# An expert layer on one core: one jump over the third block per group of weights instead of per product

## The chip, the cores and the metric

The kernel runs on one core of a Trainium2 chip. Its time is the device time in microseconds. The kernel before has a median of 1426.74 us over three runs (1427.4, 1422.75 and 1426.74).

## The reference

A trunk of two layers works on 256 tokens of width 1024, all in float32. Layer 0 is multi-scale retention and a dense SwiGLU; layer 1 is stick-breaking attention against a shared K and V, and then a mixture of eight experts. Each sub-layer ends in a layer norm over `alpha * x + f(x)`. The change is in the experts alone. There each token goes to the two experts with the largest router logits:

```python
top_val, top_idx = lax.top_k(logits, TOP_K)          # 2 of 8
gates = sum(one_hot(top_idx) * softmax(top_val))
for e in range(8):                                    # D_EXPERT = 3584
    gate, up = split(xt @ w_in[e])                    # 1024 x 7168
    y += gates[:, e] * ((silu(gate) * up) @ w_out[e]) # 3584 x 1024
```

The weights of the eight experts are 352 MB, and each is read once.

## The kernel before

Tokens are gathered per expert into 96 slots, in three blocks (`NB = 3`) of 32. An expert that has at most 64 tokens has nothing in its third block. That is known on the chip only: the router writes the flag `over[e]`, and TensorE loads it into a register (`third[e]`).

The 3584 hidden columns of an expert are worked in two units, of 2048 and 1536 (`UNITS`). For each unit `experts` runs three products: the gate and the up product (`gemm_e`, "input products", 8 weights each, a weight being 128 rows of the unit's columns) and the output product of the unit before (`down`, 16 or 12 weights of 128 rows by 1024 columns). So an expert has six products. In a product, a step is one weight: `mm_tiles` (L1102) multiplies, for each block of 32 slots, four column groups that lie side by side in the array, and each of these is two records in the profile. Between the units stand the scatter of the expert before (L1155 to L1161), and the gather of the next expert.

Weights go unsplit from HBM into slots of 1 MB. There are 18 slots in this stage (6 + 6 + 2 + 4, from four pools). A slot holds one weight of an input product (1 MB or 768 KB) or two of an output product (1 MB). All loads are issued by SP's queue (L213) in the order of use. A load waits there until the slot that it gets is given back by `done()`; `pump` hands slots to the next loads as they are given back.

`by_need` (L1105 to L1120) sets the order within a product. It takes the slots of the whole product, works the first weight with all three blocks and gives its slot back, works the other weights with the blocks 0 and 1, and then comes to one `tc.If(third > 0)` (L1118), in which the other weights are worked with block 2. Only then come the `done()` of all weights but the first. If the flag is zero, TensorE jumps over the third block's instructions. The very first product is worked weight by weight without a branch, since the flags are not loaded yet.

After the last expert follow the copies of the rows out of PSUM (L1146: blocks 0 and 1 on ScalarE, block 2 on VectorE), the last scatter, and the layer norm.

Of the kernel before, what the change touches and what calls it, by code (L numbers as in the profile page):

```python
# [24 lines left out]
KD = D // P  # L25
# [6 lines left out]
NB = 3  # L32
# [149 lines left out]
def trunk_kernel(ctx, tc, x, ret_w_in, ret_w_out, sb_w_kv, sb_w_q, sb_w_out, ln_mix_g, ln_mix_b,  # L182
# [17 lines left out]
    def wtile(name="pw"):  # L200
        return psw.tile([P, 512], F32, tag="pw", name=nm(name))
# [602 lines left out]
    def blocks(w):  # L804

        v = w.rearrange("p (b t j) -> p b t j", t=4, j=32)
        return [v[:, :, t, :] for t in range(4)]
# [13 lines left out]
    def gather_T(ps):  # L821

        xg = mp.tile([P, NB, KD, 32], F32, tag=("xgh", "xgl")[cnt_xg[0] % 2], name=nm("xg"))
        cnt_xg[0] += 1
        for r in range(NB):
            nc.vector.transpose(xg[:, r].rearrange("p k s -> p (k s)"), ps[r])
        return xg
# [14 lines left out]
    with att:  # L842
# [234 lines left out]
        xg = gather_T(first)  # L1077
# [17 lines left out]
    def mm_tiles(nb, o, lhs, cols, first, last, shared=False):  # L1095

        for r in nb:
            for c, w in enumerate(cols):
                ov = o[r][c * 32:(c + 1) * 32]
                if len(w.shape) == 3:  # L1100
                    ov = ov.rearrange("p (b j) -> p b j", j=32)
                nc.tensor.matmul(ov, lhs[r], w, start=first and not (shared and r == 1), stop=last,  # L1102
                                 skip_group_check=True)

    def by_need(s, nk, third, mm):  # L1105


        if third is None:
            for k in range(nk):
                mm(range(NB), k, s.take()[0])  # L1110
                s.done()
            return
        w = s.take(nk)
        for k in range(nk):
            mm(range(NB) if k == 0 else range(NB - 1), k, w[k])
            if k == 0:
                s.done()
        with tc.If(third > 0):  # L1118
            for k in range(1, nk):
                mm(range(NB - 1, NB), k, w[k])  # L1120
        for k in range(1, nk):
            s.done()

    def gemm_e(s, xg, n, third):


        o = [wtile("pe")[:, :n // 4] for _ in range(NB)]
        by_need(s, KD, third, lambda nb, k, w: mm_tiles(nb, o, [xg[:, r, k, :] for r in range(NB)], blocks(w),
                                                        k == 0, k == KD - 1))
        return o  # L1130

    def down(s, hT, nk, po, first, last, third):
        by_need(s, nk, third, lambda nb, k, w: mm_tiles(nb, po, [hT[:, r, k, :] for r in range(NB)],
                                                        [w[:, c * 256:(c + 1) * 256] for c in range(4)],
                                                        first and k == 0, last and k == nk - 1, True))

# [28 lines left out]
    def experts(s, pos, g, xg, norm, hook=None, most=None):  # L1165
        pend = done = po = None
        third = [None] * NE
        for e in range(NE):
            for u, (c0, n) in enumerate(UNITS):
                hs = mp2.tile([P, NB, 512], F32, tag="hs", name=nm("hs"))[:, :, :n // 4]  # L1170
                pg = gemm_e(s, xg, n, third[e])
                for r in range(NB):
                    nc.scalar.activation(hs[:, r, :], pg[r], AF.Silu)  # L1173
# [8 lines left out]
                if u == 1:  # L1182
# [3 lines left out]
                    if e + 1 < NE:  # L1186
                        g = one_hot(e + 1, pos)
                        nxt = gather(g)
                pu = gemm_e(s, xg, n, third[e])
                hT = xtp.tile([P, NB, 16, 32], F32, tag="xT_l", name=nm("hT"))[:, :, :n // P]  # L1190
                for r in range(NB):
# [3 lines left out]
                if pend is not None:  # L1195
                    if pend[1] == 0:
                        po = new_po()
                    down(s, *pend[0], po, pend[1] == 0, pend[1] == 1, third[e - (u == 0)])
                    if pend[1] == 1:
                        done = (rows_of(po), *sl)  # L1200
                pend = ((hT, n // P), u)
            if e + 1 < NE:
                xg = nxt
        down(s, *pend[0], po, False, True, third[NE - 1])
        scatter(rows_of(po), *sl, norm)

# [68 lines left out]
```

## Time and profile before

| what | value |
|---|---|
| profiled execution | 1422.93 us |
| its span | 1421.1 us |
| TensorE busy | 1349.7 us (95%) |
| mean granted TensorE clock | 0.974 |
| moved over DMA | 447.36 MB |
| expert stage | from about 537 us of the span to 1397 us |

The span goes from the first to the last instruction; the profiled execution's own time is 1.8 us longer. Times in the rows are counted from the span's start. A matmul record's line is that of the helper (L1102), so products are told apart by time, by tile (`pe` for input products, `po` for output products) and by their number of records. "PEq L1118" as a releaser is TensorE's sequencer at the branch of `by_need`.

### The profile page before, as it was taken

How to read it: one execution, taken by the hardware profiler on the slowest of the kernel's cores; microseconds unless marked ns; L12 is line 12 of the kernel's file. 1: busy time of each engine (PE TensorE's matmuls, PEld its weight loads, DVE VectorE, ACT ScalarE, POOL GpSimd, SP SyncE). 2: the span in 40 equal slices, each digit the busy share in tenths (PEclk: the TensorE clock that was granted, in tenths of full speed). 3: DMA queues.
4: the chain of work that ended last, by engine and by line, in shares of the span. 5: the costliest groups of instructions: out<-in, count | busy, mean ns of one | idle time of the engine just before them, and what ended most of it. 6: DMA issues, size and time to landing. Idle time of an engine off the chain costs nothing. (4 is left out here: it accounts for less than half of the span.)

```text
span 1421.1 us, 29884 instructions
## 1 busy us (share of the span) xinstructions
PE 1349.7 (95%) x13608; PEld 842.3 (59%) x13608; DVE 443.4 (31%) x617; ACT 314.2 (22%) x466; POOL 58.5 (4%) x80
## 2 busy tenths in 40 slices
PE   9999999999999999987989999999999999999894
PEld 7888879999989863533524444454444453443442
DVE  6746667555566570101201200200200200200204
ACT  5544425444447520001000000100100100100101
POOL 0212110000010020000000000000000000000001
PEclk9999999999999999999999999999999999999997
DMA  9864536655586356999999999989999999999960
GB/s 338 296 210 151 175 119 238 205 180 182 144 243 241 139 223 202 406 418 412 411 419 412 412 418 410 405 341 413 411 418 413 411 402 414 411 418 414 412 271 33
DMA packets 137251, 447.36 MB, mean 315 GB/s; under 512 B 9088, under 2 KB 56976, under 8 KB 120720
## 3 DMA queue, kind: packets, MB, share of 16 engines
q1 hardware_dynamic: 136144, 442.01, 80.9%
q0 software_dynamic: 960, 3.15, 0.7%
q8 instruction: 122, 2.00, 0.6%
q14 instruction: 25, 0.20, 0.0%
HBM read 444.08 MB, written 1.05 MB: 313 GB/s over the span
## 5 line engine op out<-in xcount | busy, mean ns | idle before, releaser
L1102 PE MATMUL pe<-raw,xg 128*32 128x512 f32 (+1 forms) x5304 | 513.3, 543 | 21.4 <-DMA raw<-in_moe_w_in_dram 9.6
L1102 PEld LDWEIGHTS pe<-raw,xg 128*32 128x32 f32 x5304 | 185.5, 110 | 339.6 <-issue 305.3
L1102 PE MATMUL po<-raw,hT 128*32 128x256 f32 x4544 | 249.9, 379 | 5.8 <-DMA raw<-in_moe_w_out_dram 3.3
L265 DVE TENSOR_TENSOR w<-raw,w 128x1024 fp32r<-128x1024 f32 x162 | 198.1, 1234 | 143.8 <-ACT w L264 139.8
L1102 PEld LDWEIGHTS po<-raw,hT 128*32 128x32 f32 x4544 | 158.0, 110 | 100.8 <-issue 7.4
L264 ACT CAST w<-raw 128x1024 fp32r<-128x1024 f32 x162 | 168.2, 1047 | 134.3 <-issue 32.1
L1192 DVE TENSOR_TENSOR hs<-hs,pe 128x512 f32<-128x512 f32 (+1 forms) x48 | 29.1, 620 | 384.0 <-PE pe L1102 382.6
L1173 ACT ACTIVATE hs<-pe 128x512 f32<-128x512 f32 (+1 forms) x48 | 25.4, 543 | 507.5 <-PE pe L1102 507.5
L393 PE MATMUL pf<-xT_h,w 128*128 128x256 f32 x448 | 126.9, 283 | 0.0
L395 PE MATMUL pf<-xT_l,w 128*128 128x256 f32 x448 | 126.2, 282 | 0.0
L394 PE MATMUL pf<-xT_h,w 128*128 128x256 f32 x448 | 126.1, 281 | 0.0
L1194 DVE STREAM_TRANSPOSE hT<-hs 128x512 f32<-128x512 f32 (+1 forms) x48 | 27.2, 617 | 230.0 <-PE po L1102 125.0
L393 PEld LDWEIGHTS pf<-xT_h,w 128*128 128x128 f32 x448 | 84.4, 188 | 0.3
L394 PEld LDWEIGHTS pf<-xT_h,w 128*128 128x128 f32 x448 | 84.4, 188 | 0.3
L395 PEld LDWEIGHTS pf<-xT_l,w 128*128 128x128 f32 x448 | 84.4, 188 | 0.0
L1146 ACT COPY y<-po 32x256 f32<-32x256 f32 x64 | 23.3, 364 | 258.4 <-PE po L1102 257.7
L456 POOL TENSOR_SCALAR rs<-mv 128x1 f32<-128x1 f32 x16 | 5.6, 350 | 1292.4 <-DVE mv L455 1284.5
L368 PE MATMUL pv<-w,xT_l 128*128 128x512 f32 x96 | 38.4, 400 | 0.0
L369 PE MATMUL pv<-w,xT_h 128*128 128x512 f32 x96 | 37.9, 395 | 0.0
L370 PE MATMUL pv<-w,xT_h 128*128 128x512 f32 x96 | 37.9, 395 | 0.0
L1156 DVE SCALAR_TENSOR_TENSOR yl<-y,gs,yh 96x512 fp32r<-96x512 f32 x16 | 11.9, 744 | 82.9 <-ACT yh L1155 82.8
L393 PE MATMUL pq<-xT_h,w 128*128 128x256 f32 x128 | 36.3, 283 | 0.0
(208 smaller groups left out, 1274.1 us busy)
## 6 DMA issues: line engine op xcount, KB each, us to landing
raw<-in_moe_w_in_dram SPq DMA_DIRECT2D x128, 1024.0 KB, 18.9
raw<-in_moe_w_out_dram SPq DMA_DIRECT2D x112, 1024.0 KB, 18.4
raw<-in_moe_w_in_dram SPq DMA_DIRECT2D x128, 768.0 KB, 15.2
raw<-in_ret_w_in_dram SPq DMA_DIRECT2D x22, 1024.0 KB, 9.1
raw<-in_ffn_w_in_dram SPq DMA_DIRECT2D x20, 1024.0 KB, 5.1
raw<-in_ffn_w_out_dram SPq DMA_DIRECT2D x11, 1024.0 KB, 5.0
raw<-in_ret_w_out_dram SPq DMA_DIRECT2D x8, 1024.0 KB, 5.0
raw<-in_sb_w_kv_dram SPq DMA_DIRECT2D x4, 1024.0 KB, 5.3
```

Source lines behind the costliest of these rows:

```text
L264: nc.scalar.copy(hv, v)
L265: nc.vector.tensor_sub(lv, v, hv.bitcast(F32))
L368: nc.tensor.matmul(o, sl, mh, start=first, stop=False)
L369: nc.tensor.matmul(o, sh, mh, start=False, stop=False)
L370: nc.tensor.matmul(o, sh, ml, start=False, stop=last)
L393: nc.tensor.matmul(o, lo[:, k, :], xT_h[:, k, :], start=(k == 0), stop=False)
L394: nc.tensor.matmul(o, h[:, k, :], xT_h[:, k, :], start=False, stop=False)
L395: nc.tensor.matmul(o, h[:, k, :], xT_l[:, k, :], start=False, stop=(k == KD - 1))
L1102: nc.tensor.matmul(ov, lhs[r], w, start=first and not (shared and r == 1), stop=last, skip_group_check=True)
L1173: nc.scalar.activation(hs[:, r, :], pg[r], AF.Silu)
L1192: nc.vector.tensor_mul(hs[:, r, :], hs[:, r, :], pu[r])
L1194: nc.vector.transpose(hT[:, r].rearrange("p k s -> p (k s)"), hs[:, r, :])
```

## The change

`by_need` gets a group size: 4 weights for input products and 8 for output products, which is four slots' worth in both. It goes through a product group by group. Each group is taken, worked with the blocks 0 and 1 (the product's first weight with all three), then passes a branch of its own, in which its weights are worked with block 2, and then gives its slots back. An input product has two groups of 4; an output product has two of 8, or one of 8 and one of 4. The number of matmuls and their operands stay; their order within a product changes, and a product has two branches instead of one.

```diff
@@ -1102,7 +1102,8 @@
                 nc.tensor.matmul(ov, lhs[r], w, start=first and not (shared and r == 1), stop=last,
                                  skip_group_check=True)
 
-    def by_need(s, nk, third, mm):
+    def by_need(s, nk, group, third, mm):
+
 
 
         if third is None:
@@ -1110,27 +1111,31 @@
                 mm(range(NB), k, s.take()[0])
                 s.done()
             return
-        w = s.take(nk)
-        for k in range(nk):
-            mm(range(NB) if k == 0 else range(NB - 1), k, w[k])
-            if k == 0:
+        for k0 in range(0, nk, group):
+            ks = range(k0, min(k0 + group, nk))
+            w = s.take(len(ks))
+            for k in ks:
+                mm(range(NB - (k > 0)), k, w[k - k0])
+            if k0 == 0:
                 s.done()
-        with tc.If(third > 0):
-            for k in range(1, nk):
-                mm(range(NB - 1, NB), k, w[k])
-        for k in range(1, nk):
-            s.done()
+            with tc.If(third > 0):
+                for k in ks:
+                    if k > 0:
+                        mm(range(NB - 1, NB), k, w[k - k0])
+            for k in ks:
+                if k > 0:
+                    s.done()
 
     def gemm_e(s, xg, n, third):
 
 
         o = [wtile("pe")[:, :n // 4] for _ in range(NB)]
-        by_need(s, KD, third, lambda nb, k, w: mm_tiles(nb, o, [xg[:, r, k, :] for r in range(NB)], blocks(w),
+        by_need(s, KD, 4, third, lambda nb, k, w: mm_tiles(nb, o, [xg[:, r, k, :] for r in range(NB)], blocks(w),
                                                         k == 0, k == KD - 1))
         return o
 
     def down(s, hT, nk, po, first, last, third):
-        by_need(s, nk, third, lambda nb, k, w: mm_tiles(nb, po, [hT[:, r, k, :] for r in range(NB)],
+        by_need(s, nk, 8, third, lambda nb, k, w: mm_tiles(nb, po, [hT[:, r, k, :] for r in range(NB)],
                                                         [w[:, c * 256:(c + 1) * 256] for c in range(4)],
                                                         first and k == 0, last and k == nk - 1, True))
```

## Rows read from the trace of the kernel before

**Rows 1.** Stage windows: us, busy time of each engine, TensorE clock, DMA share, GB/s.

```profile
550.00:560.00 10.00, 9.30 (x88) 3.12 (x84) 0.00 (x0) 1.77 (x3) 0.00 (x0) 1.00 0.76 240
560.00:570.00 10.00, 9.68 (x100) 3.65 (x96) 3.43 (x6) 0.00 (x0) 0.00 (x0) 1.00 0.18 46
570.00:580.00 10.00, 9.83 (x126) 4.99 (x122) 0.71 (x3) 1.79 (x5) 0.00 (x0) 1.00 1.02 419
...
1300.00:1310.00 10.00, 10.00 (x129) 3.90 (x125) 2.07 (x3) 0.00 (x0) 0.00 (x0) 1.00 1.02 414
...
1370.00:1380.00 10.00, 10.00 (x192) 5.59 (x188) 0.00 (x0) 0.00 (x0) 0.00 (x0) 1.00 0.55 191
```

**Rows 2.** TensorE's waits, 633 to 729.7 us: us in total, times, longest.

```profile
PE pe L1102 <- DMA raw<-in_moe_w_in_dram: 7.7, 13, 2.0
PE po L1102 <- DMA raw<-in_moe_w_out_dram: 3.3, 5, 0.7
```

**Rows 3.** TensorE's waits, 729.6 to 1397 us.

```profile
PE pe L1102 <- DMA raw<-in_moe_w_in_dram: 2.4, 3, 1.5
```

**Rows 4.** TensorE's timeline behind output products: start, us, what, records, idle before.

```profile
1051.59 43.10 PE L1102 MATMUL pe<-raw,xg 128*32 128x512 f32 x384 [3.15 <-PEq L1118]
...
1105.85 15.69 PE L1102 MATMUL pe<-raw,xg 128*32 128x384 f32 x192 [0.37 <-DMA raw<-in_moe_w_in_dram]
...
1263.78 3.16 PE L1102 MATMUL pe<-raw,xg 128*32 128x512 f32 x25 [0.32 <-PEq L1118]
1268.30 38.40 PE L1102 MATMUL pe<-raw,xg 128*32 128x512 f32 x356 [1.36 <-issue]
...
1319.42 15.69 PE L1102 MATMUL pe<-raw,xg 128*32 128x384 f32 x192 [1.50 <-DMA raw<-in_moe_w_in_dram]
```

**Rows 5.** Timeline of the load queue (SPq): start, us, loads, count.

```profile
567.27 2.50 SPq L213 DMA_DIRECT2D raw<-in_moe_w_in_dram  x5
...
1292.07 32.77 SPq L213 DMA_DIRECT2D raw<-in_moe_w_in_dram  x16
```

**Rows 6.** Loads of slots issued 1290 to 1332 us: time to landing.

```profile
DMA to landing us min/median/max: 14.7/16.2/19.0
```

**Rows 7.** TensorE's timeline: expert 0's second and third product, expert 2's first.

```profile
552.33 14.80 PE L1102 MATMUL pe<-raw,xg 128*32 128x512 f32 x136 [0.69 <-issue]
567.45 11.17 PE L1102 MATMUL pe<-raw,xg 128*32 128x384 f32 x136 [0.32 <-PEq L1118]
...
727.08 1.92 PE L1102 MATMUL pe<-raw,xg 128*32 128x512 f32 x16 [0.57 <-DMA raw<-in_moe_w_in_dram]
729.56 28.53 PE L1102 MATMUL pe<-raw,xg 128*32 128x512 f32 x264 [0.56 <-DMA raw<-in_moe_w_in_dram]
```

**Rows 8.** The load queue's own waits, 556 to 575 us.

```profile
SPq L213 <- PEq L1118: 11.7, 1, 11.7
```

**Rows 9.** DMA issues of the page: tensor, count, size, median us to landing.

```profile
raw<-in_moe_w_in_dram SPq DMA_DIRECT2D x128, 768.0 KB, 15.2
```

**Rows 10.** Timeline of TensorE: expert 3's first two products, in one piece.

```profile
833.73 41.39 PE L1102 MATMUL pe<-raw,xg 128*32 128x512 f32 x384
```

**Rows 11.** Timeline of TensorE: behind input products of experts 4 and 6.

```profile
1033.99 14.45 PE L1102 MATMUL po<-raw,hT 128*32 128x256 f32 x264 [0.18 <-PEq L1118]
...
1183.77 14.80 PE L1102 MATMUL pe<-raw,xg 128*32 128x512 f32 x136 [0.32 <-PEq L1118]
1199.06 15.75 PE L1102 MATMUL po<-raw,hT 128*32 128x256 f32 x288 [0.49 <-PEq L1118]
...
1249.01 14.45 PE L1102 MATMUL po<-raw,hT 128*32 128x256 f32 x264 [0.18 <-PEq L1118]
```

**Rows 12.** Timeline of all engines: copies of the last product's rows.

```profile
1392.36 3.01 ACT L1146 COPY y<-po 32x256 f32<-32x256 f32 x8 [49.54 <-PE po L1102]
1397.11 1.74 DVE L1146 COPY y<-po 32x256 f32<-32x256 f32 x4 [15.01 <-PE po L1102]
```

## The prediction

> **What bounds the kernel now.** I read the stage windows first, then TensorE's waits, then its timeline product by product, then the load queue. From about 570 us the DMA engines are saturated (share 1.02, 414 and 419 GB/s in [rows 1]), which looks like a memory bound. But a full queue does not show who is late. The waits tell it: between 633 and 729.7 us TensorE waited 7.7 + 3.3 = 11.0 us for weights [rows 2], between 729.6 and 1397 us only 2.4 us in three waits [rows 3], and even the longest of these, 1.50 us at 1319.42 [rows 4], is not for data: its product's first slot is the first of the 16 loads that begin at 1292.07 [rows 5], such loads land 14.7 to 19.0 us after issue [rows 6], so it was there by 1311; and no later slot of that product, which would land 1.9 us apart, was waited for. So there are two stretches. Until 729.56 the weight stream sets the time: slot after slot, TensorE idles for the next one (0.57 and 0.56 us in [rows 7]). From 729.56 to the end of the last product TensorE does, and what it does more or less there, and how early it gets there, is the span. The load stream ends at about 1376 (share 0.55 in the window 1370 to 1380 [rows 1]), some 20 us before TensorE.
>
> A product of 192 records (8 weights x 3 blocks x 4 columns x 2) ran the third block, one of 136 jumped over it. By that count experts 0, 1, 4 and 6 jump, and 2, 3, 5 and 7 don't.
>
> **The change part by part.**
> *Earlier loads.* Expert 0's second product starts at 552.33 and ends at 567.1 [rows 7]. Its slots are full, and the queue waits 11.7 us for the branch behind the product [rows 8]; then, at 567.27, five loads go out within 2.50 us [rows 5], and the DMA share of 560 to 570 is 0.18 [rows 1]. With the change the first group of four weights is done after 24 + 3 x 16 = 72 records of 14.80/136 = 0.109 us, so at 560.2, and three slots come free (the first already came free alone). Three loads of 768 KB = 0.786 MB [rows 9] at 415 GB/s ([rows 1]) are 5.7 us of transfer, and fit into the 7 us to 567.3. The queue then never runs dry: four more slots follow at 567.3 (8.8 us of loads), and the next product gives back halves too. The stream is 5.7 us further from there. The cover for this is the 11.0 us that TensorE waits before 729.56: these can shrink by 5.7, with a few new jumps (0.3 each, below) also inside them. Bounds: 0, if the three loads don't get out earlier, and 5.7, since there are only three slots. I take 5.7.
>
> *Blocks done while waiting.* Expert 2's first product runs the third block and waits for its weights. Now the last weight begins at 729.56, and behind it come two blocks and then seven third blocks. With groups, the third blocks of the weights 1 to 3 are done behind weight 3, while weights 4 to 7 still come in: three blocks of 8 x 28.53/264 = 0.865 us [rows 7], 2.6 us, are taken out from behind the last landing. They fit: weights 4 to 7 need 1.72 us of TensorE each at a landing every 2.5 us, so the 2.6 us is made up again before the last one. The product's end goes from 729.56 + 1.73 + 7 x 0.865 = 737.3 to about 729.0. The stream stays close for the next three products: the next one's last weight lands at 729.56 - 5.7 + 8 x 2.5 = 743.9, and TensorE comes to it at 729.0 + 2.6 + 3 x 1.73 + 2.6 + 3 x 1.73 = 744.6, which leaves 0.7 us. Bounds 0 and 2.6; I take 2.6. So TensorE gets to its own stretch 5.7 + 2.6 = 8.3 us earlier.
>
> *More jumps.* A product that runs its third block shows no gap at its branches: 384 records of two products in one piece, 41.39 us [rows 10], 0.108 us each as in a waitless stretch. So the added branches of experts 2, 3, 5 and 7 cost nothing, bound 0.3 each. A jump taken costs 0.18, 0.32, 0.49 and 0.18 us behind input products [rows 11], mean 0.3. These jump over 7 weights x 4 columns x 4 = 112 instructions (two records, each with its weight load). Each input product of experts 4 and 6 has one jump more (over 48, then 64): 8 x 0.3 = +2.4 us, all on the path. Those of experts 0 and 1 are in the first stretch, under the waits.
>
> *Shorter jumps.* Behind the output products, which jump over 15 x 16 = 240 or 11 x 16 = 176 instructions, the gaps are another thing [rows 4]: 3.15 us (expert 4), 0.37, then 0.32 and 1.36 a little later (expert 6), and 1.50. The 3.15 us also left TensorE slower: the next 384 records took 43.10 us instead of 41.39, 1.7 us more. Sum 3.15 + 1.7 + 0.37 + 1.68 + 1.50 = 8.4 us. With the change each becomes two jumps over 112 and 128, or 112 and 64, instructions. By the nearest rows, those of 112, that is 4 x 2 x 0.3 = 2.4 us: a gain of 6.0. The other end: the stalls stay as they are and each product has one short jump more, 4 x 0.3 = 1.2 us lost. I take the 6.0, since length is what differs between the two sets of rows, and keep both ends.
>
> [...]
>
> *The tail.* In the last product the copies of the first two blocks' rows (3.01 us on ScalarE) begin at 1392.36, under the last eleven third blocks; the third block's copies begin at 1397.11 [rows 12]. With groups of 8 and 4 the first two blocks end only four third blocks before the end, 4 x (1397.11 - 1392.36)/11 = 1.7 us, so ScalarE's copies end 0.4 us later than VectorE's first half does now: +0.4 us.
>
> **Sum.** -5.7 - 2.6 + 2.4 - 6.0 + 0.4 = -11.5 us on the profiled execution's 1422.93, 1411.4. The timed runs lie between 1422.75 and 1427.4, median 1426.74, so that execution is at their lower end, 3.8 below the median. I put half of this on top: 1413.
>
> **Rivals.**
> 1. *The long stalls are not of the length.* Then +1.2 instead of -6.0: 1418.6, and 1420.5 with half the difference to the median. For it: the four gaps of the output products differ among themselves by a factor of eight. Against: none of the rows of 112 comes near.
> 2. *The stream is not moved.* The three slots don't come back before the branch at the product's end, or the loads only wait later. Then -2.6 + 2.4 - 6.0 + 0.4 = -5.8: 1417.1, 1419 with the half. That is also the case in which the change does not do what it says. For it: a slot's return follows a branch, and how that is counted no row shows. Against: the returns at 567.27 follow the branch directly.
> 3. *Slower: every jump stalls.* If a branch in the middle of a product meets instructions not yet there, the 24 jumps of experts 4 and 6 (16 in input products, 8 in output products) cost what the long ones do now, (3.15 + 0.37 + 1.68 + 1.50)/4 = 1.7 us: 24 x 1.7 = 40 us, instead of the 2.4 + 6.7 = 9.1 that these products' jumps cost now. +31 - 8.3 + 0.4 = +23, 1446. It turns from faster to slower at (9.1 + 8.3 - 0.4)/24 = 0.7 us per jump. For it: there are twice as many jumps. Against: no jump over 112 instructions costs more than 0.49.
>
> **How the numbers follow.** Forecast 0.5, rival 1 0.22, rival 2 0.13, rival 3 and what lies between it and rival 1 0.15. A measurement of this kernel tells about 0.3%, 4.3 us, from no change, so faster means under 1422.5. The forecast and both first rivals are under it, with about a tenth of their chance not, by the spread of the runs. Of the last 0.15 a half is slower than 1431. Faster 0.78, the same 0.13, slower 0.09. The likeliest case's own range is 1406 to 1418; low end 1406 if the clock drops behind stalls (1.7 us at one of them) go elsewhere too; high end 1425 takes in rivals 1 and 2 and the start of the third.
>
> **What would show it.** Right: the DMA share of 560 to 570 well over half; no run of waits for weights in the second half of expert 2's first product, and its end near 729 instead of 737.3; experts 4 and 6 with two gaps of about 0.3 us in each product and none over 1 us; two-product pieces of 384 records still without a gap. Wrong: the share at 560 still near 0.2 (rival 2), gaps over 1 us behind the output products (rival 1) or in the middle of products (rival 3), or new waits for weights after 770, which would say that TensorE has caught the stream and part of the 11.5 us stays there.

## The result: 1419.47 us, 7 us under before

The changed kernel takes 1419.47 us (median of 7 runs, 1418.51 to 1420.67) against 1426.68 us for the kernel before (7 runs); the ratio is 0.995, with an interval of 0.994 to 0.996. The forecast of 1413 us had the direction and, as the experiments show, the mechanism of the earlier loads; its size was nearly twice what came. The time is that of the first rival (1418.6 to 1420.5), but by luck: the terms of its sum are not the ones that were measured, as the part on the prediction shows.

The stage windows of the changed kernel (columns as in [rows 1]) show the weight stream where it was idle before:

```profile
550.00:560.00 10.00, 9.32 (x92) 3.04 (x87) 0.00 (x0) 1.79 (x3) 0.00 (x0) 1.00 0.86 273
560.00:570.00 10.00, 9.62 (x88) 3.02 (x80) 0.78 (x2) 0.00 (x0) 0.00 (x0) 1.00 0.72 274
570.00:580.00 10.00, 9.72 (x120) 4.62 (x124) 3.37 (x7) 0.00 (x0) 0.00 (x0) 1.00 0.92 344
```

From 560 to 570 us the DMA share is 0.72, where it was 0.18. TensorE's waits for weights follow, first those of 633 to 730 us, then those of 729.6 to 1397 us (us in total, times, longest):

```profile
PE pe L1102 <- DMA raw<-in_moe_w_in_dram: 2.1, 6, 0.4
PE po L1102 <- DMA raw<-in_moe_w_out_dram: 0.4, 1, 0.4
...
PE pe L1102 <- DMA raw<-in_moe_w_in_dram: 1.6, 1, 1.6
PE po L1102 <- DMA raw<-in_moe_w_in_dram: 0.3, 1, 0.3
```

In the first stretch 11.0 us [rows 2] have become 2.5. TensorE's timeline shows the places that answer to [rows 4, 7, 10]:

```profile
709.74 16.66 PE L1102 MATMUL pe<-raw,xg 128*32 128x512 f32 x144 [0.31 <-PEq L1121]
726.71 25.96 PE L1102 MATMUL pe<-raw,xg 128*32 128x512 f32 x240 [0.30 <-DMA raw<-in_moe_w_in_dram]
...
765.12 11.82 PE L1102 MATMUL pe<-raw,xg 128*32 128x384 f32 x144 [1.27 <-PEq L1121]
778.51 4.08 PE L1102 MATMUL pe<-raw,xg 128*32 128x384 f32 x48 [1.58 <-DMA raw<-in_moe_w_in_dram]
...
830.67 41.39 PE L1102 MATMUL pe<-raw,xg 128*32 128x512 f32 x384
...
1047.80 41.41 PE L1102 MATMUL pe<-raw,xg 128*32 128x512 f32 x384 [0.30 <-PEq L1121]
...
1100.69 15.69 PE L1102 MATMUL pe<-raw,xg 128*32 128x384 f32 x192 [0.32 <-PEq L1121]
...
1256.73 5.56 PE L1102 MATMUL po<-raw,hT 128*32 128x256 f32 x97 [0.47 <-issue]
1263.10 41.41 PE L1102 MATMUL pe<-raw,xg 128*32 128x512 f32 x384 [0.81 <-PEq L1121]
...
1316.18 15.69 PE L1102 MATMUL pe<-raw,xg 128*32 128x384 f32 x192 [0.30 <-PEq L1121]
...
1396.20 0.50 PE L1164 MATMUL psc<-yh,gT 96*128 96x512 f32 x1 [2.15 <-ACT yh L1160]
```

Expert 2's first product (from 709.74) runs 144 records before its only wait, 0.30 us for the last weight. The 3.15 us behind expert 4's first unit are 0.30 now (1047.80), the 1.50 at the end are 0.30 (1316.18). But other gaps stand there: 1.27 us at 765.12, then a wait of 1.58 us for a weight at 778.51, and 0.47 and 0.81 us around 1260, where before had 0.32 and 1.36 [rows 4]. Expert 2's third product (an expert's input products are counted from first to fourth), which has the wait, was not free of gaps in before either:

```profile
769.21 1.45 PE L1102 MATMUL pe<-raw,xg 128*32 128x384 f32 x10 [0.33 <-PEq L1118]
771.16 15.04 PE L1102 MATMUL pe<-raw,xg 128*32 128x384 f32 x182 [0.49 <-issue]
```

A product that runs its third block still has no gap at its branches (830.67).

The profiled execution took 1420.67 us, 2.3 less than that of before, although the medians differ by 7.2. Part of that is ahead of the change: expert 0's second product starts at 554.61 here and at 552.33 in [rows 7]. So from here on places are counted from the start of that product. The start of each product is found in every run by counting the records of the trace, since the number of records of each product is known:

| kernel | expert 2, second product starts | expert 2, first output product starts | expert 4 starts | expert 6 starts | last product ends |
|---|---|---|---|---|---|
| before (us) | 185.0 | 260.7 | 401.1 | 616.3 | 844.7 |
| before, profiled again | +0.1 | +0.7 | +0.8 | +1.0 | +0.7 |
| changed | -7.7 | -5.3 | -5.0 | -6.3 | -5.3 |
| e0_only | -4.9 | -4.2 | -3.7 | -3.3 | -3.4 |
| in_only | -7.6 | -6.5 | -6.3 | -6.6 | -5.1 |
| out_only | +0.1 | +1.1 | +1.6 | +0.8 | +2.3 |
| shift_before | +0.8 | +1.2 | +1.3 | -1.9 | -2.7 |
| e2_only | -2.5 | +1.0 | +1.5 | +1.9 | +1.8 |
| early_in | -7.8 | -5.5 | -5.1 | -7.9 | -5.5 |
| finer | -8.0 | -5.9 | -5.8 | -3.5 | -3.4 |
| shift_256 | -0.1 | +0.9 | +1.6 | +2.1 | +2.1 |
| shift_after | -6.8 | -5.6 | -5.4 | -3.4 | -2.5 |
| e0_fine | -6.5 | -5.9 | -5.6 | -6.3 | -7.9 |
| early_in_long | -7.5 | -4.9 | -5.0 | -6.4 | -4.5 |

Every line after the first is that kernel's time less that of the first line, from one profiled execution each.

### The profile page after: what moved, and what is told of

It reads as the page before. It is cut to its first block, busy times and chain, and to the rows that moved or that the text cites. A ratio compares the mean times of both kernels' runs of the same rounds, so it can differ in the third digit from the quotient of the medians.

```text
span 1418.8 us, 30029 instructions
## 1 busy us (share of the span) xinstructions
PE 1353.8 (95%) x13608; PEld 849.3 (60%) x13608; DVE 443.4 (31%) x617; ACT 314.1 (22%) x466; POOL 58.6 (4%) x80
## 3 DMA queue, kind: packets, MB, share of 16 engines
q0 software_dynamic: 960, 3.15, 0.7%
## 5 line engine op out<-in xcount | busy, mean ns | idle before, releaser
L1102 PEld LDWEIGHTS pe<-raw,xg 128*32 128x32 f32 x5304 | 189.9, 111 | 329.7 <-issue 301.1
L1102 PEld LDWEIGHTS po<-raw,hT 128*32 128x32 f32 x4544 | 160.9, 110 | 98.3 <-issue 12.2
L1161 DVE SCALAR_TENSOR_TENSOR yl<-y,gs,yh 96x512 fp32r<-96x512 f32 x16 | 11.9, 744 | 85.6 <-ACT yh L1160 85.6
L817 PE MATMUL pgx<-x,g 128*32 128x256 f32 x384 | 34.7, 531 | 2.3 <-DVE x L492 1.1
```

Of the source, the lines that this page charges most:

```text
L817: nc.tensor.matmul(ps[r][c * 32:(c + 1) * 32].rearrange("p (b j) -> p b j", j=32), g[:, t, r * 32:(r + 1) * 32], x_, start=(t == 0 and r ! ...
```

## The experiments

All kernels but the repeat have the changed kernel's `by_need`; two functions give the group size of each product (`u` is the unit, `up` is 1 for the up product). With a group as large as the product the order is that of the kernel before.

```diff
+def group_in(e, u, up):    # input products, 8 weights
+    return 4
+def group_out(e, u):       # output products, 16 or 12 weights
+    return 8
-    def gemm_e(s, xg, n, third):
+    def gemm_e(s, xg, n, third, group):
-        by_need(s, KD, 4, third, ...
+        by_need(s, KD, group, third, ...
```

| kernel | median us | kernel before beside it | ratio, interval |
|---|---|---|---|
| e0_only | 1420.08 | 1425.75 | 0.9967 (0.9955 to 0.9979) |
| in_only | 1419.44 | 1425.75 | 0.9958 (0.9943 to 0.9973) |
| out_only | 1424.38 | 1425.75 | 0.9988 (0.9975 to 1.0001) |
| shift_before | 1423.21 | 1425.75 | 0.9980 (0.9971 to 0.9989) |
| e2_only | 1424.48 | 1425.83 | 0.9988 (0.9978 to 0.9998) |
| early_in | 1417.77 | 1425.83 | 0.9943 (0.9927 to 0.9958) |
| finer | 1423.99 | 1425.83 | 0.9987 (0.9976 to 0.9998) |
| shift_256 | 1429.03 | 1424.75 | 1.0026 (1.0013 to 1.0038) |
| shift_after | 1422.98 | 1424.75 | 0.9981 (0.9970 to 0.9993) |
| e0_fine | 1418.66 | 1424.75 | 0.9957 (0.9942 to 0.9973) |
| early_in_long | 1418.43 | 1424.75 | 0.9952 (0.9934 to 0.9970) |

**The earlier loads alone (e0_only).**

```diff
-    return 4
+    return 4 if (e, u, up) == (0, 0, 1) else 8
-    return 8
+    return 16
```

> Only one product is grouped: the second input product of expert 0 (two groups of four); all others keep one branch. Theory A (the weight stream starts earlier): DMA share of the ten us in the middle of that product from 0.2 to about 0.7, the weights of expert 1 and of expert 2's first product land 5 to 6 us earlier, waits for weights before expert 2's second product fall from 11 to about 6 us, time 5 us under the kernel before (1421 to 1423). No third block is taken out from behind a landing, so not the 7 us of the full change. Rival B (the gain lies in the shorter jumps of the output products): no difference to the kernel before, within 1 us.

Its stage window of 560 to 570 us, and of its TensorE timeline the last weight of expert 2's first product:

```profile
560.00:570.00 10.00, 9.51 (x100) 3.59 (x100) 3.22 (x6) 0.00 (x0) 0.00 (x0) 1.00 0.77 271
```

```profile
724.45 28.53 PE L1110 MATMUL pe<-raw,xg 128*32 128x512 f32 x264 [0.57 <-DMA raw<-in_moe_w_in_dram]
```

The share is 0.77, and the last weight's work begins at 724.45 - 552.16 = 172.3 us after the count's start, against 729.56 - 552.33 = 177.2 [rows 7]: 4.9 us earlier. The time is 5.7 us under the kernel before, near the 5 of theory A, and by one branch in one product: the gaps behind the output products of experts 4 and 6 are those of before (their stretches, as summed in the part on the prediction, take 101.0 us here and 101.1 there). The rival that all is in the output products falls.

**Input products alone, output products alone (in_only, out_only).** First the edit of in_only, then that of out_only:

```diff
     return 4
-    return 8
+    return 16
```

```diff
-    return 4
+    return 8
     return 8
```

> All input products in groups of four, output products with one branch as before. Theory A: stream 5 us, third blocks of expert 2 2.6 us, eight more jumps of 0.36 us in experts 4 and 6 (+2.9), long gaps behind output products as before: 5 us under the kernel before. Rival B: 3 us slower than the kernel before, since only the extra jumps remain.

> Output products in groups of eight, input products with one branch as before. Theory A: no earlier loads (share 0.2 in the idle ten us), the gaps behind the output products of experts 4 and 6 shrink from 6.7 to 2.4 us and one slow stretch goes: 3 to 6 us under the kernel before. Rival B: 7 us under, the whole of the gain. Rival C (a stall depends on where the target lies in the instruction stream, not on the length of the jump): gaps over 1 us still appear, behind other products than before, and the time is within 3 us of the kernel before.

The input products bring 6.3 us (5 expected), the output products 1.4 us, with an interval that just takes in no change; theory A had 3 to 6 for them. Behind expert 4's and expert 6's first output products the TensorE timeline of out_only shows:

```profile
1054.62 1.92 PE L1110 MATMUL pe<-raw,xg 128*32 128x512 f32 x16 [1.15 <-PEq L1129]
...
1271.14 40.96 PE L1110 MATMUL pe<-raw,xg 128*32 128x512 f32 x377 [1.54 <-issue]
```

These jumps go over 112 and 128 instructions, like those behind the input products, and gaps over 1 us stand behind them nevertheless. That is against the length, and for the place.

**The same code 128 and 256 instructions further on (shift_before, shift_256), and the kernel before profiled again.** First the edit of shift_before; in shift_256 the 64 is 128. The last number is the width of the result, a parameter that `keep_warm` gets for this. Both group sizes are those of the kernel before.

```diff
         keep_warm(WARM[0], wm[:, 0:128], wm)
+        keep_warm(64, wm[:, 0:128], wm[:, 0:8], 8)
```

> The kernel before with 64 tiny matmuls (128 instructions with their weight loads) more at its start, where TensorE waits for x; every later instruction of TensorE lies 128 further on in its stream. If the gaps of over 1 us behind the output products come from the length of the jump, the same ones (expert 4's first unit, expert 6's both) show again, and the time is within 2 us of the kernel before plus what the start costs (at most 4 us). Rival C: the gaps over 1 us stand behind other products, and the sum of the gaps differs by some us.

> The kernel before, unchanged, for a second profile. It shows what differs between two executions of the same instructions. If the gaps of over 1 us behind output products belong to places in the instruction stream, they stand behind the same products and agree within 0.5 us; if they are chance (a fetch beside a full weight queue), they move. The stretch before the experts and the slower clock behind the scatters may differ by 2 to 4 us, which would explain that the timed runs spread over 6 us.

> The kernel before with 128 tiny matmuls (256 instructions) more at its start. With 128 instructions more the long gaps moved to other output products. Theory C (a gap stands where a jump's target falls in the blocks by which TensorE's instructions are fetched): if such a block is 256 instructions, the pattern of the kernel before comes back, 3.2 us behind expert 4's first unit, 1.9 behind expert 0's second, 1.0 to 1.5 behind both of expert 6, and the time is within 2 us of the kernel before. If the block is another size, the gaps stand behind yet other products.

TensorE's timeline, behind the output products of experts 4 and 6. First the kernel before in its second profile:

```profile
1053.51 43.10 PE L1102 MATMUL pe<-raw,xg 128*32 128x512 f32 x384 [3.33 <-PEq L1118]
...
1269.74 38.40 PE L1102 MATMUL pe<-raw,xg 128*32 128x512 f32 x356 [0.97 <-issue]
...
1320.84 4.40 PE L1102 MATMUL pe<-raw,xg 128*32 128x384 f32 x52 [1.48 <-PEq L1118]
```

Then with 128 instructions more (the first line is behind expert 1):

```profile
717.31 3.57 PE L1111 MATMUL pe<-raw,xg 128*32 128x512 f32 x16 [3.93 <-PEq L1130]
...
1051.58 41.65 PE L1111 MATMUL pe<-raw,xg 128*32 128x512 f32 x384 [0.32 <-PEq L1130]
...
1264.94 41.41 PE L1111 MATMUL pe<-raw,xg 128*32 128x512 f32 x384 [2.00 <-PEq L1130]
...
1317.46 8.87 PE L1111 MATMUL pe<-raw,xg 128*32 128x384 f32 x103 [0.32 <-PEq L1130]
```

And with 256 more:

```profile
1058.68 43.10 PE L1111 MATMUL pe<-raw,xg 128*32 128x512 f32 x384 [3.22 <-PEq L1130]
...
1275.25 38.40 PE L1111 MATMUL pe<-raw,xg 128*32 128x512 f32 x356 [1.04 <-issue]
...
1326.51 3.75 PE L1111 MATMUL pe<-raw,xg 128*32 128x384 f32 x44 [1.64 <-DMA raw<-in_moe_w_in_dram]
```

The second profile of before has its gaps at the same products as [rows 4], within 0.4 us. With 128 instructions more they are at others: nothing at expert 4's and at expert 6's second, 2.00 us behind expert 6's first, and 3.93 us behind expert 1, where TensorE waits for weights anyway. With 256 more the first pattern is back. So a gap belongs to the place of the code in TensorE's instruction stream, and in these runs the pattern comes back when the code is moved by 256 instructions, and not when it is moved by 128.

The profile has DMA queues that it names `instruction`; this is the one whose packets are all of 16.4 KB (packets, MB, share of the 16 engines): first all of before, then before from 1048.5 to 1051.5 us, inside its gap of 3.15 us:

```profile
q8 instruction: 122, 2.00, 0.6%
...
q8 instruction: 1, 0.02, 2.3%
```

That one packet ends at 1049.90, and TensorE goes on at 1051.59, 1.7 us later. It is 1.7 us again in the second profile of before and behind expert 1 in shift_before, and 1.8 in shift_256; in shift_before, whose gap at expert 4's is 0.32 us, no such packet lies between 1048.5 and 1051.6. Over all fourteen profiles, from 800 to 1330 us, there are 29 gaps over 0.75 us between two matmuls of weights, apart from the one ahead of expert 4's second product, where the kernel loads a register (0.74 us in before, 0.82 in e0_fine). All of them end 1.2 to 1.8 us after the end of a packet of this queue; of the 180 gaps of 0.15 to 0.6 us 14 do. That holds for gaps right at a branch and for those some records behind it, like the 1.36 us of [rows 4]. What no run here shows is what such a packet holds, nor why the gap stands behind a jump at one place and not at another.

One more thing is seen in the same lines: in the two kernels with the 3.2 us gap, the 384 records behind it take 43.10 us, in the one without it 41.65.

The price of a place: with 128 instructions more and no other difference the kernel before gains 2.5 us in the time. In shift_256 the time is 4.3 us over, more than the 2 expected: its first projection matmul begins at 10.63 us and not at 7.67, so the added matmuls themselves cost 3.0 us.

**The blocks done while waiting, alone (e2_only).**

```diff
-    return 4
+    return 4 if (e, u, up) == (2, 0, 0) else 8
-    return 8
+    return 16
```

> Only the first input product of expert 2 (the one that waits for its weights and runs its third block) is in two groups of four. Theory A: that product ends 2.6 us earlier, with the weights landing as before. But the weights are no earlier, so the next product, in one group, waits for its last weight: it has 0.7 us of room, so about 2 of the 2.6 us are lost again within expert 2, and the time is 0.5 to 1 us under the kernel before. If nothing is lost, the time is 2.6 us under it. Rival B (only shorter jumps of output products count): the product does not end earlier.

The TensorE timeline of the end of expert 2's first product, all of its second, and the start of what follows:

```profile
731.28 16.84 PE L1110 MATMUL pe<-raw,xg 128*32 128x512 f32 x152 [0.45 <-DMA raw<-in_moe_w_in_dram]
748.70 1.92 PE L1110 MATMUL pe<-raw,xg 128*32 128x512 f32 x16 [0.58 <-DMA raw<-in_moe_w_in_dram]
751.22 7.93 PE L1110 MATMUL pe<-raw,xg 128*32 128x512 f32 x72 [0.59 <-DMA raw<-in_moe_w_in_dram]
758.97 10.97 PE L1110 MATMUL po<-raw,hT 128*32 128x256 f32 x200
```

The first product ends 2.5 us earlier (2.6 expected), and the second one, which waited for no weight in the kernel before, waits twice for 0.6 us and takes 1.9 us longer (22.5 against 20.6). So about 0.5 of the 2.5 us is left behind it. That the kernel is 1.0 us behind at the output product has another source: from the start of expert 2's third product to that of its fourth, with the scatter in between, it takes 29.9 us, and 28.3 and 28.9 in the two profiles of before. The time is 1.3 us under before (0.5 to 1 expected).

**Fewer jumps and more (early_in, finer).** First the edit of early_in, then that of finer:

```diff
-    return 4
+    return 4 if e < 3 else 8
```

```diff
-    return 4
+    return 2 if e in (4, 6) else 4
```

> As the changed kernel, but from expert 3 on the input products have one branch again. Theory A: the early part is as in the changed kernel; the input products of experts 4 and 6 together lose 3.2 us (eight jumps of 0.4) less, so 3 us under the changed kernel, apart from gaps over 1 us behind output products, which may stand elsewhere and change this by 3 us either way. If a jump in the middle costs nothing on the path: no difference in the input products of 4 and 6.

> As the changed kernel, but the input products of experts 4 and 6 are in four groups of two. Sixteen jumps more, each over 16 or 32 instructions; the sum of instructions jumped over is the same. If a jump costs 0.4 us whatever its length: the input products of 4 and 6 take 6.4 us longer than in the changed kernel (0.8 us each), and the time is 6 us over it. If the cost goes with the instructions jumped over: no difference.

By the same count, the stretches from the start of expert 4, and of expert 6, to the start of its first output product hold the four input products of each. The two together take 160.9 us in before, 163.7 in the changed kernel, 160.9 in early_in and 170.5 in finer. So against early_in the eight jumps more of the changed kernel cost 2.8 us, and the sixteen more of finer another 6.8 us: 0.35 to 0.42 us each, over 16 instructions as over 64. The TensorE timeline of finer in expert 6's first product shows the same:

```profile
1172.34 3.64 PE L1110 MATMUL pe<-raw,xg 128*32 128x512 f32 x32 [0.18 <-PEq L1129]
1176.15 3.64 PE L1110 MATMUL pe<-raw,xg 128*32 128x512 f32 x32 [0.17 <-PEq L1129]
1179.96 3.64 PE L1110 MATMUL pe<-raw,xg 128*32 128x512 f32 x32 [0.17 <-PEq L1129]
```

A group of 32 records starts every 3.81 us, while 32 records in an unbroken piece take 32 x 41.39/384 = 3.45 us [rows 10]: 0.36 us a jump, half of it inside the row and not in the gap. early_in is the fastest kernel here by its median, 1417.77 us, and beats the kernel before; it is 1.7 us under the changed kernel (3 expected), and their intervals meet. finer is 4.5 us over the changed kernel (6 expected).

**The changed kernel at another place, and three more versions (shift_after, e0_fine, early_in_long).** The edits: the 64 tiny matmuls in the changed kernel; groups of two in expert 0; and early_in with undivided output products.

```diff
+        keep_warm(64, wm[:, 0:128], wm[:, 0:8], 8)
```

```diff
-    return 4
+    return 2 if e == 0 else 4 if e < 3 else 8
```

```diff
-    return 4
+    return 4 if e < 3 else 8
-    return 8
+    return 16
```

> The changed kernel with 128 instructions more at its start. Theory C: its gaps over 0.8 us (behind expert 1's second unit 1.27, behind expert 6's first 0.81) go elsewhere, others appear, and the time is within 3 us of the changed kernel on either side. If the gaps of the changed kernel have to do with short jumps alone, they stay.

> Input products in groups of two in expert 0, of four in experts 1 and 2, undivided from expert 3 on; output products in groups of eight. Against the same kernel with groups of four in expert 0: slots come back two at a time, the weight stream gets up to 2 us further, the wait of 1.6 us for the last weight of expert 2's third product goes; the extra jumps of expert 0 (0.4 us each) are covered by waits. 1 to 2 us under that kernel, 10 us under the kernel before. If the stream is not the bound there any more: no difference.

> Input products in groups of four in experts 0 to 2, undivided from expert 3 on, output products with one branch. Against the same kernel with output products in groups of eight: each of the four output products of experts 4 and 6 has one jump of 0.4 us less, and gaps over 1 us stand where the jump's place in the stream puts them. By the failed term of the prediction (short jumps take the gaps away) it would be 6 us slower; by theory C within 3 us on either side.

In shift_after the gaps of the changed kernel are gone and others stand elsewhere; its TensorE timeline behind the first units of experts 1 and 4:

```profile
712.00 3.21 PE L1111 MATMUL pe<-raw,xg 128*32 128x512 f32 x28 [1.11 <-PEq L1130]
...
1050.52 2.04 PE L1111 MATMUL pe<-raw,xg 128*32 128x512 f32 x16 [1.55 <-issue]
```

It takes 1422.98 us, and shift_before 1423.21: at this place the change is worth next to nothing. The table shows where it goes. At expert 4's start the changed code is 6.7 us ahead (-5.4 against +1.3), at the end 0.2 behind (-2.5 against -2.7); what lies ahead of the count, as the start that is 1.2 us later in shift_after's profile, has no part in this. The added jumps of experts 4 and 6 take 3.0 us of that (by the stretches as above), and the four output products of these experts 4.7 us, because at this place the long jumps happen to be the cheap ones (next part); the rest gives 0.8 us back. early_in_long, with long jumps, is 0.7 us over early_in: within 3 us, as theory C had it, and not 6. e0_fine moved its profile by the 2 us expected (-7.9 at the end against -5.5 in early_in), with no weight waited for in expert 2's third product, but its median is 0.9 us over early_in's and not under it: no difference that these runs can tell.

## Why the prediction came out too large, step by step

- *TensorE sets the time from 729.56 on, the stream before.* Right. e0_only moves the loads alone and shortens the kernel by 5.7 us; the waits that covered it shrank from 11.0 us to 6.2 there (about 6 expected) and to 2.5 in the changed kernel.
- *Earlier loads, -5.7.* Measured -4.9 at expert 2's second product (e0_only). The mechanism was right. The share of 560 to 570 is 0.77 there and not near 1; from 550 to 580 the stream moved 236, 271 and 415 GB/s against 240, 46 and 419 in before, 2.2 MB more, which is 5.2 us at 415 GB/s.
- *Blocks done while waiting, -2.6.* Right where it was looked for: 2.5 us in e2_only. Between e0_only and the changed kernel it is 2.8, which holds the other groups of experts 0 and 1 too. But the 7.7 us were not kept: at expert 2's first output product 5.3 are left. The prediction had nothing in its sum for this. Of the 2.4 us 1.3 are in expert 1's second output product: it stands behind expert 2's second product, where TensorE sets the time, and has a jump more and a gap of 1.27 us in place of 0.33. The prediction had put the jumps of expert 1 under the waits. Another 0.5 is in the product behind it. It waits 1.58 us for a weight at 778.51, the sign that the prediction had named (a wait for weights after 770); but it takes 17.5 us, as in the second profile of before, and 17.0 in the first. The last 0.5 is around the scatter that follows.
- *More jumps, +2.4.* 2.8 (0.35 to 0.42 each). The gaps of [rows 11] hold only about half of a jump's cost; the rest is in the row before it.
- *Shorter jumps, -6.0.* This is the step that failed, by the reason that it gave: "length is what differs between the two sets of rows". What differs is the place. Take the output products of experts 4 and 6, and with each first one the input product behind it, which a slow stretch can lengthen, each from its start to the start of the next product. The sum is 101.1 and 100.8 us in the two profiles of before. With short jumps it is 96.7 in the changed kernel, 100.0 in shift_after, 99.9 in out_only, 100.5 in early_in and 95.6 in finer; with long jumps it is 95.3 at another place, in shift_before, and 99.5 in in_only and 101.2 in early_in_long. So the gain here was 4.4 us and not 6.0, and it is one of place: short jumps reach from 95.6 to 100.5 and long ones from 95.3 to 101.2. The first rival, with 0.22, had the mechanism right, that the long stalls are not of the length. Its size, +1.2, was not: the stalls did not stay, they moved, and here to the kernel's advantage.
- *The tail, +0.4.* Right: the first scatter matmul behind the last product waits 2.15 us (1396.20 above), and 1.78 in before.
- *Products that run the third block: no cost.* Right (830.67 above).
- *The other rivals.* The second falls with the share of 0.72, the third, whose "instructions not yet there" was the author's assumption, with the 0.35 to 0.42 us of a jump.
- *Half of the 3.8 us on top.* The profiled execution of before, 1422.93, was a low one: 26 later runs lie between 1422.15 and 1428.85, median 1425.75, and the second profile was at 1424.5. So against the median the forecast was 13.7 us and 7.2 came.

By these sizes, -4.9 - 2.8 + 2.4 + 2.8 - 4.4 = -6.9 us, where the profile has -5.3 at the last product's end. The remaining 1.6 us stand in the last input products of experts 3, 5 and 7 and the scatters ahead of them. From the end of expert 5's third product to the start of its fourth, for one, it is 11.8 us and 10.9 in before, and from 10.2 to 11.9 over the other kernels. What sets this stays open: in the 16 us from that scatter's first matmul the mean granted clock is 0.79 in both, and nothing was tried to steer it. How much the change is worth free of the places is also open: between the two places tried it is 7.2 and 0.2 us.

## What to carry to other kernels

A full DMA queue over a whole stage (share 1.02 here, with 2.4 us of waits for weights from 729.6 us on) does not say that weights bound it: look for the one place where the stream stood still (share 0.18 from 560 to 570 us), and for who came late afterwards. There a buffer given back half a product earlier was worth more (4.9 us) than any other part of this change, and one branch in one product did it. Where a branch costs what it did here, 0.35 to 0.42 us, put it where a wait covers it, and before a gain of 0.3% is put down to an edit of code with jumps, move the same code by some instructions (128 of them were worth 2.5 us here) and time it again.

## What the runs showed of the hardware that was not expected

- A gap of 1 to 4 us behind a jump stands at the same products in two executions of a kernel (3.15 and 3.33 us at expert 4's), goes to others or changes its length when the code is moved by 128 instructions (0.32 us there), and comes back when it is moved by 256 (3.22 us). The time of the kernel before went from 1425.75 to 1423.21 us by 128 instructions that do nothing.
- Such a gap ends 1.2 to 1.8 us after the end of a packet of 16.4 KB on the instruction queue (all 29 gaps over 0.75 us between matmuls of weights from 800 to 1330 us in fourteen profiles, but for the one at a register load).
- A jump costs 0.35 to 0.42 us whether it goes over 16 or 64 instructions; the profile's gap in the middle of a product shows 0.17 to 0.18 of it.
- Behind a gap of 3.15 to 3.93 us ahead of two products in one piece their 384 records took 43.01 to 43.10 us, in each of the seven profiles that have one; behind 0.30 to 1.63 us it was 41.41 to 41.68. In between it went both ways (43.10 behind 2.23 us, 41.41 behind 2.00 and 2.54), so such a gap can cost 1.7 us more than it shows. In before the mean granted clock from 1050 to 1060 us is 0.83, with 1.00 in the ten us on either side.
